# Partial sums of a seven-product pair kept in PSUM banks instead of added one by one

## The chip, the cores and the metric

The kernel runs on one core of a Trainium2 chip. The metric is the device time of one execution in microseconds. Engines are named as in the profile: PE is TensorE (matrix products), PEld its weight loads, DVE VectorE, ACT ScalarE, POOL GpSimd, SP SyncE, which issues most transfers.

## The reference

One layer of a diffusion backbone over 128 context and 1024 latent tokens (T = 1152), width 1024, fp32. Cut to what matters here:

```python
h = rmsnorm(x, g_norm_mix) * (1 + sc1) + sh1
z = h @ w_in                       # latents, gates, q/k/v of the mLSTM, output and branch gates
...                                # latent attention (A) and bidirectional mLSTM (B)
out = (g_a * (att @ w_o_mla) + g_b * (hm @ w_o_mlstm)) @ w_out
x = x + gt1 * out
h = rmsnorm(x, g_norm_ffn) * (1 + sc2) + sh2
a, u = split(h @ w_ffn_in, 2)      # 2 x 2816 features
x = x + gt2 * ((silu(a) * u) @ w_ffn_out)
```

The change concerns `h @ w_in` (all but a few of its columns) and `h @ w_ffn_in`.

## The kernel before

Features lie on the 128 partitions, tokens along the free dimension. Each fp32 operand is split into a high part (`hi`, ACT, line 69) and a low part (`lo`, DVE, line 75), and a product is made of three matmuls, high by high, high by low, low by high (`mm3`, lines 98 to 100).

`pair` (line 1645) computes two tiles of 128 output features for column groups of 576 tokens, as a 2 by 2 block product: the blocks of the weights are two tiles by two halves of K (a11, a12, a21, a22), those of the moving side two halves of K by two halves of 288 tokens (B11 to B22). Seven block products take the place of eight (Winograd's form). The stationary operands, `a` blocks or sums S1 to S4 of them, are formed by `w_ops` (from line 1620): POOL forms the sums (lines 1632, 1633, 1638, 1642, tile `ws`), ACT and DVE split each (tile `wo`, 4 buffers in the first product and 6 in the feed-forward product). The moving operands T1 to T4 and the B blocks are formed once and serve all pairs; for the feed-forward product `h2_ops` does that for one half of the tokens (normalization at line 1572, modulation at 1578, sums on POOL from 1590 on, splits).

The table `ORDER` (line 1616) names what step i of a pair multiplies. In every step, for each column group, twelve matmuls of 128x288 (4 blocks of K, three matmuls each) fill one bank of the pool `mm`, which has six banks in both products. The bank is read by one instruction per sum it enters: the first product is copied by ACT (line 1670, tile `m`), the other six steps add theirs on DVE (helper `add`, line 1658) to what is there, with two additions in step 3, seven in all:

```python
elif i == 1: add(u2[g], m1[g], b)
elif i == 2: add(d[g][1], u2[g], b)
elif i == 3: add(d[g][2], u2[g], b); add(d[g][3], d[g][1], b)
elif i == 4: add(d[g][0], m1[g], b)
elif i == 5: add(d[g][1], d[g][1], b)
else: add(d[g][2], d[g][2], b); done(g)
```

`pair` is called 19 times with two column groups by the first product (`z_lat`, `z_qk`, `z_big`; from 184 to 650 us), and for the 22 pairs of the feed-forward product, each a gate and a value tile: pairs 0 to 5 first for tokens 0 to 575 alone, then for the others alone, while `h2_ops` of the second half of the tokens is still at work, then pairs 6 to 21 with both groups (from 1425 to 1950 us). In `z_big` the outputs are tiles `zo`; `done` takes their sigmoid (line 660) and a DVE multiplication (662). In the feed-forward product they are `sa` and `uu`; `done` takes silu of `sa` (ACT, line 1702), multiplies (POOL, 1703) and stores.

Beside the pairs runs other work, of which `tick` emits a piece per step. In `z_big` it is `background` (line 666), modulation columns: per piece a DVE multiplication with sum (line 700, `mj`), a POOL multiplication (701) and an ACT sum (682, `wm`); at its start and halfway a vector `sr` is loaded and ACT takes its silu (689). The compiler's scheduler then orders the instructions of each engine; each engine works its queue off in order.

## Time and profile before

| what | value |
|---|---|
| median of 3 runs (lowest, highest) | 2245.0 us (2242.07, 2249.43) |
| span of the profiled execution, first to last instruction | 2242.8 us |
| mean granted TensorE clock | 0.966 |
| PE busy | 2083.1 us, 93% |
| DVE busy | 1659.5 us, 74%, 2998 instructions |
| ACT busy | 1068.0 us, 48%, 2225 instructions |
| POOL busy | 1127.2 us, 50% |

The profiled execution lists its span alone; the median of the runs is 2.2 us above it. A busy share is an average over stages in which different engines set the pace; the views by stretch, the waits and the chain tell which one does where.

### The profile page before, as it was taken

Reading aid. Unit: us, or ns where it says so; the run is one execution under the profiler, and the core shown is the slowest. Engines: PE = TensorE matmul, PEld = TensorE weight load, DVE = VectorE, ACT = ScalarE, POOL = GpSimd, SP = SyncE. Lnnn points to the kernel's source line nnn. Section 1 sums busy time; section 2 is a strip of 40 time slices with the busy share of each in tenths; the row PEclk is TensorE's granted clock in tenths of the full one; section 3 lists DMA queues with packets and bytes.
Section 4 is the critical chain, followed back from the end, with each engine's and each line's share of the span. In section 5 each row is a group of like instructions: output and inputs, shape, how many; then the busy total and the mean of one; then the engine's idle time right before and its main releaser. Section 6 shows DMA issues by size and latency. Waiting matters only on the chain.

```text
span 2242.8 us, 40186 instructions
## 1 busy us (share of the span) xinstructions
PE 2083.1 (93%) x14713; PEld 1998.2 (89%) x14713; DVE 1659.5 (74%) x2998; ACT 1068.0 (48%) x2225; POOL 1127.2 (50%) x850
## 2 busy tenths in 40 slices
PE   6799999999989987999999999879999999989898
PEld 2799998999978776998998999879999999989897
DVE  6725745988845879998987666899755565799895
ACT  4322333445445556777776435444322222356464
POOL 3612122667624415877877543677867634431411
PEclk8899999999999998999999999999999999999899
DMA  7121244555479775322224575223555522557664
GB/s 286 63 93 59 90 142 124 164 174 183 152 241 330 238 230 175 90 74 65 84 66 102 170 224 157 86 83 122 186 177 183 175 89 80 161 173 248 206 201 138
DMA packets 234532, 340.97 MB, mean 152 GB/s; under 512 B 18110, under 2 KB 170398, under 8 KB 233310
## 3 DMA queue, kind: packets, MB, share of 16 engines
q1 hardware_dynamic: 225790, 328.73, 46.0%
q0 software_dynamic: 4848, 6.06, 1.1%
q10 hardware_dynamic: 3696, 3.61, 0.5%
q8 instruction: 116, 1.90, 0.4%
q14 instruction: 82, 0.67, 0.1%
HBM read 250.55 MB, written 87.80 MB: 151 GB/s over the span
## 4 chain that ended last, share of the span: by engine, by line
PE 42%; DVE 16%; DMA 7%; POOL 6%; issue 6%; ACT 2%; SPq 1%; DVEq 0%; POOLq 0%; ACTq 0%
PE mm L98 10%; PE mm L100 10%; PE mm L99 10%; DVE wo L75 4%; DMA pr<-w_fo 3%; DVE sm L1374 2%; DVE pl L75 1%; PE st L98 1%; PE pv L1437 1%; PE pv L1438 1%; PE st L100 1%; PE st L99 1%; PE mx L1372 1%; DMA N<-d_nm 1%; PE p L1079 1%
## 5 line engine op out<-in xcount | busy, mean ns | idle before, releaser
L100 PE MATMUL mm<-th,wo 128*128 128x288 f32 x1840 | 546.8, 298 | 14.0 <-DVE wo L75 13.7
L98 PE MATMUL mm<-th,wo 128*128 128x288 f32 x1840 | 547.6, 298 | 2.7 <-DVE zo L1658 1.1
L99 PE MATMUL mm<-tl,wo 128*128 128x288 f32 x1840 | 546.2, 297 | 0.0
L100 PEld LDWEIGHTS mm<-th,wo 128*128 128x128 f32 x1840 | 348.9, 190 | 18.2 <-DVE wo L75 17.6
L75 DVE TENSOR_TENSOR wo<-wr,wo 128x512 fp32r<-128x512 f32 (+1 forms) x317 | 314.6, 1008 | 59.4 <-ACT wo L69 54.4
L98 PEld LDWEIGHTS mm<-th,wo 128*128 128x128 f32 x1840 | 348.2, 189 | 4.5 <-issue 1.6
L99 PEld LDWEIGHTS mm<-tl,wo 128*128 128x128 f32 x1840 | 348.3, 189 | 0.1
L69 ACT ACTIVATE wo<-wr 128x512 fp32r<-128x512 f32 (+1 forms) x317 | 187.5, 607 | 147.9 <-PE mm L100 69.5
L69 ACT ACTIVATE wo<-ws 128x512 fp32r<-128x512 f32 x188 | 116.7, 627 | 271.7 <-PE mm L100 160.5
L75 DVE TENSOR_TENSOR wo<-ws,wo 128x512 fp32r<-128x512 f32 x188 | 186.7, 996 | 62.1 <-ACT wo L69 61.9
L100 PE MATMUL mm<-xh,wo 128*128 128x288 f32 x616 | 184.7, 301 | 10.3 <-DVE wo L75 10.3
L1642 POOL TENSOR_TENSOR ws<-wr,ws 128x512 f32<-128x512 f32 x47 | 62.3, 1326 | 243.5 <-DVE wo L75 238.2
L99 PE MATMUL mm<-xl,wo 128*128 128x288 f32 x616 | 184.7, 300 | 0.0
L98 PE MATMUL mm<-xh,wo 128*128 128x288 f32 x616 | 184.2, 299 | 0.5 <-ACT wo L69 0.5
L1420 POOL TENSOR_TENSOR es<-es,p 128x512 f32<-128x512 f32 (+1 forms) x96 | 129.4, 1348 | 34.8 <-ACT p L1403 19.9
L98 PE MATMUL mm<-B,wo 128*128 128x288 f32 x456 | 134.8, 296 | 2.6 <-DVE zo L1658 1.7
L100 PE MATMUL mm<-B,wo 128*128 128x288 f32 x456 | 134.8, 296 | 0.0
L99 PE MATMUL mm<-B,wo 128*128 128x288 f32 x456 | 134.8, 296 | 0.0
L701 POOL TENSOR_TENSOR wm<-wm,sr 128x512 f32<-128x512 f32 x64 | 100.1, 1567 | 65.2 <-DVE mj L700 49.2
L100 PEld LDWEIGHTS mm<-xh,wo 128*128 128x128 f32 x616 | 118.1, 192 | 12.7 <-DVE wo L75 12.5
L98 PEld LDWEIGHTS mm<-xh,wo 128*128 128x128 f32 x616 | 118.2, 192 | 0.7 <-ACT wo L69 0.7
L99 PEld LDWEIGHTS mm<-xl,wo 128*128 128x128 f32 x616 | 118.4, 192 | 0.0
(443 smaller groups left out, 6076.6 us busy)
## 6 DMA issues: line engine op xcount, KB each, us to landing
wr<-w_ff SPq DMA_DIRECT2D x56, 512.0 KB
wm<-wm SPq DMA_DIRECT2D x32, 512.0 KB
wr<-d_w SPq DMA_DIRECT2D x32, 512.0 KB
d_z<-zo SPq DMA_DIRECT2D x48, 288.0 KB
d_g<-uu SPq DMA_DIRECT2D x44, 288.0 KB
wr<-w_big SPq DMA_DIRECT2D x24, 512.0 KB
wr<-w_fo SPq DMA_DIRECT2D x24, 512.0 KB
pr<-w_fo SPq DMA_DIRECT2D x40, 256.0 KB
```

What stands on the lines that cost most here:

```text
L69: i = self.nc.scalar.activation(out, in_, AF.Copy)
L75: return self.nc.vector.tensor_sub(out, in_, f32v(hi)).ins
L98: mm(out, lhs[0], rhs[0], start=first, stop=False)
L99: mm(out, lhs[0], rhs[1], start=False, stop=False)
L100: self.pe = mm(out, lhs[1], rhs[0], start=False, stop=last).ins
L701: nc.gpsimd.tensor_tensor(w[:, n], w[:, n], sr[:, 1], op=ALU.mult)
L1079: self.pe = mm(p1, A[:, h], V[:, h], start=True, stop=not carried).ins
L1372: nc.tensor.matmul(s[:, :kc], q[0:QK, 0, q0 + t * P:q0 + (t + 1) * P], k[0:QK, 0, k0 + j * kc:k0 + (j + 1) * kc], start=True, stop=True)
L1374: nc.vector.tensor_reduce(sm[:, 3 * t + j:3 * t + j + 1], s[:, :kc], axis=AX.X, op=ALU.max, negate=True)
L1420: G.tensor_tensor(U["sum"][:, :m], U["sum"][:, :m], p[:, :m], op=ALU.add)
L1437: nc.tensor.matmul(pv[:, :n], v[:, i], ph[:, e, :n], start=c + e == 0, stop=False)
L1642: G.tensor_tensor(s4, a12, s2, op=ALU.subtract)
```

## The change

The seven products are computed in another order, and those that are summed anyway accumulate in the same bank. Steps 0, 2, 4 and 6 of a column group share a bank X, steps 1 and 3 a bank Y, step 5 has its own. X and Y are copied out by ACT while they hold a partial sum: X after step 0 (`m`), after step 2 (into output 1) and after step 6 (output 2), Y after step 1 (`y`). DVE adds Y to output 1 after step 3, `y` and X to output 3 after step 4, `m` and step 5's bank to output 0. The matmuls are as many as before.

```diff
-    ORDER = (("A11", "B11"), ("S2", "T2"), ("S1", "T1"), ("S3", "T3"), ("A12", "B21"), ("S4", "B22"), ("A22", "T4"))
+    ORDER = (("A11", "B11"), ("S1", "T1"), ("S2", "T2"), ("S4", "B22"), ("S3", "T3"), ("A12", "B21"), ("A22", "T4"))
...
         yield split(a11)
+        yield split(s1)
         yield split(s2)
-        yield split(s1)
+        s4 = s()
+        G.tensor_tensor(s4, a12, s2, op=ALU.subtract)
+        yield split(s4)
         s3 = s()
         G.tensor_tensor(s3, a11, a21, op=ALU.subtract)
         yield split(s3)
         yield split(a12)
-        s4 = s()
-        G.tensor_tensor(s4, a12, s2, op=ALU.subtract)
-        yield split(s4)
         yield split(a22)
...
+        def keep(to, b, n):
+            to[g] = sp.tile([P, HT], F32, name=self.nm(n), tag="u2", bufs=self.ub)
+            nc.scalar.copy(to[g], b)
...
-                b = self.bank(self.pp, "mm")[:, :HT]
+                if i in (0, 1):
+                    (X, Y)[i][g] = bank()
+                b = bank() if i == 5 else (Y if i in (1, 3) else X)[g]
                 for k in range(4):
-                    self.mm3(b, (w[:, 0, k], w[:, 1, k]), (h[:, k], l[:, k]), k == 0, k == 3)
+                    self.mm3(b, (w[:, 0, k], w[:, 1, k]), (h[:, k], l[:, k]), k == 0 and i in (0, 1, 5), k == 3, skip=True)
                 if i == 0:
-                    m1[g] = sp.tile([P, HT], F32, name=self.nm("m1"), tag="u2", bufs=self.ub)
-                    nc.scalar.copy(m1[g], b)
+                    keep(m1, b, "m1")
                 elif i == 1:
-                    u2[g] = sp.tile([P, HT], F32, name=self.nm("u2"), tag="u2", bufs=self.ub)
-                    add(u2[g], m1[g], b)
+                    keep(y1, b, "y1")
                 elif i == 2:
                     d[g] = dst(g)
-                    add(d[g][1], u2[g], b)
+                    nc.scalar.copy(d[g][1], b)
                 elif i == 3:
-                    add(d[g][2], u2[g], b)
-                    add(d[g][3], d[g][1], b)
+                    add(d[g][1], d[g][1], b)
                 elif i == 4:
+                    add(d[g][3], y1[g], b)
+                elif i == 5:
                     add(d[g][0], m1[g], b)
-                elif i == 5:
-                    add(d[g][1], d[g][1], b)
                 else:
-                    add(d[g][2], d[g][2], b)
+                    nc.scalar.copy(d[g][2], b)
                     done(g)
```

In `h2_ops` the split of B22 moves ahead of that of T3, and the split of B21 ahead of that of T4:

```diff
         split("T2", t1)
+        split("B22", b22)
+        self.free(s22)
         split("T3", b12)
         self.free(s12)
-        split("B22", b22)
-        self.free(s22)
         G.tensor_tensor(t1, b21, t1, op=ALU.subtract)
+        split("B21", b21)
+        self.free(s21)
         split("T4", t1)
         self.free(st1)
-        split("B21", b21)
-        self.free(s21)
```

The second feed-forward product, which has an order of its own, is left alone.

The order of instructions shows the change in three places. First PE, in the feed-forward product's pairs with one column group, late in that part: the first of the twelve matmuls of each step (`mm` with its number is the bank's tile, `th` the moving operand, `wo` the stationary one). Before, one pair:

```order
L98 MATMUL mm_18100<-th_16945,wo_18097 128x288 [waits DVE_49,Activation_49]
...
L98 MATMUL mm_18118<-th_16956,wo_18115 128x288 [waits DVE_49,Activation_49]
...
L98 MATMUL mm_18136<-th_16950,wo_18133 128x288 [waits DVE_49,Activation_49]
...
L98 MATMUL mm_18157<-th_16960,wo_18154 128x288 [waits DVE_49,Activation_49]
...
L98 MATMUL mm_18175<-th_16973,wo_18172 128x288 [waits DVE_49,Activation_49]
...
L98 MATMUL mm_18194<-th_16964,wo_18191 128x288 [waits DVE_49,Activation_49]
...
L98 MATMUL mm_18211<-th_16969,wo_18208 128x288 [waits Activation_49]
```

Now, beginning with step 0 of a pair (tile `mm_17870` is its bank X, `mm_17888` its Y, `mm_17960` its step 5; `mm_17736` is bank X of the pair before, `mm_18004` and `mm_18022` are X and Y of the next):

```order
L98 MATMUL mm_17870<-th_16755,wo_17867 128x288
...
L98 MATMUL mm_17888<-th_16760,wo_17885 128x288 [waits Activation_49]
...
L98 MATMUL mm_17736<-th_16783,wo_17840 128x288 [waits DVE_49]
...
L98 MATMUL mm_17870<-th_16766,wo_17903 128x288 [waits Activation_49]
...
L98 MATMUL mm_17888<-th_16770,wo_17923 128x288 [waits Activation_49]
...
L98 MATMUL mm_17960<-th_16779,wo_17957 128x288
...
L98 MATMUL mm_17870<-th_16774,wo_17941 128x288 [waits Activation_49]
...
L98 MATMUL mm_18004<-th_16755,wo_18001 128x288
...
L98 MATMUL mm_18022<-th_16760,wo_18019 128x288 [waits Activation_49]
...
L98 MATMUL mm_17870<-th_16783,wo_17974 128x288 [waits DVE_49]
```

Before, the steps stand in their own order, each in a new tile. Now step 6 of the pair before comes after step 1, step 5 after step 3, and the next pair's steps 0 and 1 before step 6; between two uses of a bank lie two steps or more. The waits that stand at matmuls of these steps are for ACT and DVE. In the parts with two column groups the steps stay in their own order, each for both groups, with the matmuls of three other group-steps between two uses of a bank.

Second DVE, at the same place. Before, most of one pair (`u` the first sum, `sa` and `uu` the outputs):

```order
L1658 TENSOR_TENSOR u_3451_18131<-m_3448_18113,mm_18118 128x288 [waits PE_49]
L75 TENSOR_TENSOR wo_18236<-wr_18228,wo_18236 128x512 [waits DMAHW4_49,Activation_49]
L1658 TENSOR_TENSOR sa_18149<-u_3451_18131,mm_18136 128x288 [waits DVE_49,PE_49]
L75 TENSOR_TENSOR wo_18254<-ws_18233,wo_18254 128x512 [waits Activation_49]
L1658 TENSOR_TENSOR uu_18150<-u_3451_18131,mm_18157 128x288 [waits DMAHW2_49,PE_49]
L1658 TENSOR_TENSOR uu_18150<-sa_18149,mm_18157 128x288 [waits DVE_49]
L75 TENSOR_TENSOR wo_18272<-ws_18232,wo_18272 128x512 [waits Activation_49]
L1658 TENSOR_TENSOR sa_18149<-m_3448_18113,mm_18175 128x288 [waits PE_49]
L75 TENSOR_TENSOR wo_18293<-ws_18291,wo_18293 128x512 [waits Activation_49]
L1658 TENSOR_TENSOR sa_18149<-sa_18149,mm_18194 128x288 [waits DVE_49,PE_49]
L75 TENSOR_TENSOR wo_18311<-wr_18228,wo_18311 128x512 [waits Activation_49]
L1658 TENSOR_TENSOR uu_18150<-uu_18150,mm_18211 128x288 [waits PE_49]
```

Now:

```order
L1659 TENSOR_TENSOR uu_17785<-y_3247_17767,mm_17736 128x288 [waits DMAHW0_49,PE_49]
L75 TENSOR_TENSOR wo_17941<-ws_17939,wo_17941 128x512 [waits Activation_49]
L75 TENSOR_TENSOR wo_17957<-wr_17859,wo_17957 128x512 [waits DVE_49,PE_49,Activation_49]
L75 TENSOR_TENSOR wo_17974<-wr_17861,wo_17974 128x512 [waits DVE_49,DMAHW2_49,PE_49,Activation_49]
L75 TENSOR_TENSOR wo_18001<-wr_17993,wo_18001 128x512 [waits DMAHW4_49,PE_49,Activation_49]
L75 TENSOR_TENSOR wo_18019<-ws_17997,wo_18019 128x512 [waits PE_49,Activation_49]
L1659 TENSOR_TENSOR sa_17918<-sa_17918,mm_17888 128x288 [waits PE_49]
L75 TENSOR_TENSOR wo_18037<-ws_17998,wo_18037 128x512 [waits Activation_49]
L1659 TENSOR_TENSOR uu_17919<-y_3267_17901,mm_17870 128x288 [waits DMAHW3_49,PE_49]
L1659 TENSOR_TENSOR sa_17918<-m_3264_17883,mm_17960 128x288 [waits PE_49]
L75 TENSOR_TENSOR wo_18057<-ws_18055,wo_18057 128x512 [waits Activation_49]
```

Between the splits of the weights (line 75) seven additions stood per pair; now there are three (line 1659 in the changed kernel), `sa` twice and `uu` once.

Third ACT, in the `z_big` pair in which the second `sr` is loaded. Before (1670 the copy of the first product, one per column group):

```order
L69 ACTIVATE wo_5158<-ws_5156 128x512 [waits PE_49,Activation_49]
L660 ACTIVATE zo_4866<-zo_4866 128x576 [waits DVE_49]
L1670 COPY m_727_5056<-mm_5043 128x288 [waits PE_49]
L1670 COPY m_729_5071<-mm_5058 128x288 [waits PE_49]
L69 ACTIVATE wo_5197<-wr_5032 128x512 [waits Activation_49]
L682 ACTIVATE wm_4945,ms<-wm_4945 128x512 [waits DMAHW4_49,Activation_49,Pool_49]
L682 ACTIVATE wm_4945,ms<-wm_4945 128x512 [waits Pool_49]
L69 ACTIVATE wo_5234<-ws_5232 128x512 [waits PE_49,Activation_49]
L689 ACT_TABLE_LOAD [waits DMAHW2_49]
L689 ACTIVATE sr_5110<-sr_5110 128x1024 [waits DVE_49]
L69 ACTIVATE wo_5271<-wr_5034 128x512 [waits DMAHW1_49,PE_49,Activation_49]
```

Now (1663 copies `m` and `y`, 1682 copies the second partial sum into output 1):

```order
L1663 COPY m_631_4936<-mm_4923 128x288 [waits PE_49]
L682 ACTIVATE wm_4829,ms<-wm_4829 128x512 [waits DMAHW4_49,Pool_49]
L1663 COPY m_633_4951<-mm_4938 128x288 [waits PE_49]
L69 ACTIVATE wo_5073<-ws_5071 128x512
L682 ACTIVATE wm_4829,ms<-wm_4829 128x512 [waits Pool_49]
L1663 COPY y_637_4973<-mm_4960 128x288 [waits PE_49]
L689 ACT_TABLE_LOAD [waits DMAHW2_49]
L689 ACTIVATE sr_4990<-sr_4990 128x1024 [waits DVE_49]
L1663 COPY y_639_4988<-mm_4975 128x288 [waits PE_49]
L69 ACTIVATE wo_5106<-wr_4912 128x512
L1682 COPY zo_5014<-mm_4923 128x288 [waits DMAHW6_49,PE_49]
L1682 COPY zo_5028<-mm_4938 128x288 [waits DMAHW5_49,DMAHW0_49,PE_49]
```

Two copies per pair became eight, of which six stand here; they alternate with instructions that wait for POOL (682), and the silu of `sr` (689), which waits for a load, now stands between the two copies of `y`.

## Rows read from the trace of the kernel before

**Rows 1.** The page's line of busy time by engine (us, share of the span, instructions), and its chain of waits summed by engine.

```profile
PE 2083.1 (93%) x14713; PEld 1998.2 (89%) x14713; DVE 1659.5 (74%) x2998; ACT 1068.0 (48%) x2225; POOL 1127.2 (50%) x850
...
PE 42%; DVE 16%; DMA 7%; POOL 6%; issue 6%; ACT 2%; SPq 1%; DVEq 0%; POOLq 0%; ACTq 0%
```

**Rows 2.** Busy time by stretch: start and end, length, then for PE, PEld, DVE, ACT and POOL the busy us with the instructions in brackets, the granted TensorE clock as a share of full speed, DMA share, GB/s. 440 to 540 is the part of the first product that has background work beside it, 1435 to 1520 the first pairs of the feed-forward product, 1600 to 1920 its later pairs, 1920 to 2000 its end.

```profile
440.00:540.00 100.00, 93.44 (x691) 91.46 (x690) 87.16 (x150) 52.24 (x115) 67.95 (x46) 1.00 0.55 175
490.00:515.00 25.00, 21.73 (x158) 20.86 (x158) 19.14 (x34) 13.70 (x28) 14.96 (x11) 1.00 0.52 163
1435.00:1520.00 85.00, 71.08 (x479) 67.13 (x478) 84.25 (x103) 43.40 (x73) 53.98 (x29) 0.94 0.28 87
1600.00:1920.00 320.00, 318.86 (x2386) 317.95 (x2385) 178.51 (x303) 87.68 (x157) 183.31 (x174) 1.00 0.43 138
1920.00:2000.00 80.00, 70.81 (x504) 68.98 (x503) 69.78 (x66) 38.95 (x64) 41.63 (x16) 0.96 0.60 185
```

**Rows 3.** The same view for the instructions of line 1658 alone, the additions of the partial sums: length, DVE busy us (instructions), clock, DMA share, GB/s.

```profile
440.00:540.00 100.00, 22.77 (x57) 1.00 0.55 175
1435.00:1520.00 85.00, 15.21 (x36) 0.94 0.28 87
1920.00:2000.00 80.00, 7.80 (x18) 0.96 0.60 185
```

**Rows 4.** Instructions of line 1658 (one of its ten groups) and of line 1670, the copy of the first product: count, duration in ns (shortest/median/longest), first and last start.

```profile
L1658 DVE TENSOR_TENSOR u<-m,mm x82: 437/442/456, 188.5 to 1932.2; 128x288 f32<-128x288 f32 x82
...
L1670 ACT COPY m<-mm x82: 375/398/405, 184.7 to 1928.3; 128x288 f32<-128x288 f32 x82
```

**Rows 5.** The chain of waits in 1435 to 1520, its shares by engine and line (the row ends where the view cuts it).

```profile
by line: DVE wo L75 35.0%; issue 19.6%; DVE x L1572 7.4%; DVE tl L75 6.2%; DVE dg L141 5.3%; DVE sa L1658 5.2%; DVE uu L1658 4.7%; PE mm L100 3.7%; PE mm L99 2.7%; PE mm L98 2.7%; DVE u L1658 1.8%; DVE t L122 1.6%; ACT th L69 1.3%; ACT sa L
```

**Rows 6.** What TensorE waited for (us in total, times, longest us), in 440 to 540, in 1435 to 1520 and in 1600 to 1920, in this order, parted by dots.

```profile
PE mm L98 <- DVE zo L1658: 2.8, 3, 1.5
PE mm L100 <- DVE wo L75: 2.8, 4, 1.3
...
PE mm L100 <- DVE wo L75: 10.4, 6, 5.5
...
PE mm L98 <- DVE sa L1658: 0.5, 1, 0.5
```

**Rows 7.** VectorE's instructions with two operands from SBUF in 1435 to 1520, by line and form: count, busy us, mean ns, idle time before them.

```profile
L75 DVE TENSOR_TENSOR wo<-ws,wo 128x512 fp32r<-128x512 f32 x20 | 25.0, 1267 | 0.3 <-ACT wo L69 0.3
L75 DVE TENSOR_TENSOR wo<-wr,wo 128x512 fp32r<-128x512 f32 x15 | 20.6, 1394 | 0.0
L75 DVE TENSOR_TENSOR tl<-x,th 128x1152 fp32r<-128x1152 f32 x4 | 8.5, 2130 | 0.0
L1572 DVE TENSOR_TENSOR x<-x,acc 128x1152 f32<-128x1152 f32 x4 | 6.3, 1623 | 0.0
...
L75 DVE TENSOR_TENSOR tl<-t,th 128x1152 fp32r<-128x1152 f32 x3 | 5.6, 1861 | 0.2 <-ACT th L69 0.2
```

**Rows 8.** The timeline of VectorE and, behind the dots, of GpSimd around 1500: start us, duration us, engine, line, operation (x2: two behind each other).

```profile
1493.89 0.44 DVE L1658 TENSOR_TENSOR u<-m,mm 128x288 f32<-128x288 f32 x1
...
1497.41 3.15 DVE L75 TENSOR_TENSOR wo<-ws,wo 128x512 fp32r<-128x512 f32 x1
...
1504.98 1.34 DVE L75 TENSOR_TENSOR tl<-t,th 128x1152 fp32r<-128x1152 f32 x1
...
1506.62 1.28 DVE L75 TENSOR_TENSOR wo<-ws,wo 128x512 fp32r<-128x512 f32 x2
...
1492.70 2.54 POOL L1703 TENSOR_TENSOR uu<-uu,sa 128x576 f32<-128x576 f32 x1
...
1496.90 3.12 POOL L1600 TENSOR_TENSOR t<-x,t 128x1152 f32<-128x1152 f32 x1
...
1508.04 1.29 POOL L1642 TENSOR_TENSOR ws<-wr,ws 128x512 f32<-128x512 f32 x1 [4.62 <-DVE wo L75]
```

**Rows 9.** What ScalarE waited for (us in total, times, longest us) in 360 to 650 and, behind the dots, in 1420 to 1560.

```profile
ACT wm L682 <- POOL wm L701: 77.5, 48, 3.9
...
ACT L689 <- DMA sr<-cR: 3.6, 1, 3.6
...
ACT sa L1702 <- DVE sa L1658: 26.5, 9, 6.1
ACT wo L69 <- POOL ws L1633: 11.6, 4, 4.2
```

**Rows 10.** The timeline of ScalarE at 498 to 506 and, behind the dots, at 1440 to 1448 (in square brackets the idle time before, and what ended it).

```profile
498.64 1.28 ACT L689 ACT_TABLE_LOAD   x1 [3.58 <-DMA sr<-cR]
499.93 1.06 ACT L689 ACTIVATE sr<-sr 128x1024 f32<-128x1024 f32 x1
500.89 0.61 ACT L69 ACTIVATE wo<-wr 128x512 fp32r<-128x512 f32 x1
503.11 0.63 ACT L682 ACTIVATE wm<-wm 128x512 f32<-128x512 f32 x1 [1.60 <-POOL wm L701]
...
1440.83 0.68 ACT L1702 ACTIVATE sa<-sa 128x576 f32<-128x576 f32 x1 [1.86 <-DVE sa L1658]
...
1445.20 2.19 ACT L1578 ACTIVATE x<-x,mod,A 128x288 f32<-128x288 f32 x4 [2.04 <-DVE x L1572]
...
1447.81 2.17 ACT L1578 ACTIVATE x<-x,mod,A 128x288 f32<-128x288 f32 x4
```

More of the change, by code (lines that the diff above doesn't have):

```diff
@@ L93, in load_w, with mm3 @@
         return (h.rearrange("p (k f) -> p k f", k=kt), l.rearrange("p (k f) -> p k f", k=kt))
-    def mm3(self, out, lhs, rhs, first, last):
+    def mm3(self, out, lhs, rhs, first, last, skip=False):
         mm = self.nc.tensor.matmul
-        mm(out, lhs[0], rhs[0], start=first, stop=False)
-        mm(out, lhs[0], rhs[1], start=False, stop=False)
-        self.pe = mm(out, lhs[1], rhs[0], start=False, stop=last).ins
+        mm(out, lhs[0], rhs[0], start=first, stop=False, skip_group_check=skip)
+        mm(out, lhs[0], rhs[1], start=False, stop=False, skip_group_check=skip)
+        self.pe = mm(out, lhs[1], rhs[0], start=False, stop=last, skip_group_check=skip).ins
     def gemm_tile(self, w, x, evac, pool, tag, chunks=CHUNKS, m=P, f0=0):
@@ L1654, in pair @@
             r.append(t)
-        m1, u2, d = {}, {}, {}
+        m1, y1, d, X, Y = {}, {}, {}, {}, {}
+        bank = lambda: self.bank(self.pp, "mm")[:, :HT]
         def add(*args):
             self.ev = nc.vector.tensor_add(*args).ins
+        def keep(to, b, n):
+            to[g] = sp.tile([P, HT], F32, name=self.nm(n), tag="u2", bufs=self.ub)
+            nc.scalar.copy(to[g], b)
         for i, w in enumerate(self.w_ops(*r)):
```

## The prediction

> **What bounds the kernel now.** I read the page first: TensorE is busy 93% of the span, VectorE 74%, ScalarE 48%, and the chain that ended last lies on TensorE for 42% and on VectorE for 16% of its length [rows 1]. An average like this does not tell what fewer additions are worth, so I read the stretches in which `pair()` runs. They differ. From 1600 to 1920 TensorE is busy 318.9 of 320 us and VectorE only 178.5: there the products set the time, and no VectorE work taken away can show. From 1435 to 1520, the first feed-forward pairs, it is the other way round: VectorE is busy 84.25 of 85 us and TensorE 71.1. From 440 to 540 TensorE is busy 93.4 of 100 us with VectorE at 87; half of the 6.6 us lost lie in 490 to 515, where 21.7 of 25 are busy [rows 2]. From 1920 to 2000 TensorE misses 9.2 us, but only 18 additions still run there, against 36 in 1435 to 1520 and 57 in 440 to 540 [rows 2, 3]. The reader is to see that the change can only pay in the first feed-forward pairs and in the background part of the first product.
>
> What TensorE waits for there agrees: 10.4 us for the low parts of the weights (line 75) in 1435 to 1520; in 440 to 540 2.8 us for those and 2.8 us for additions that had not yet read their bank [rows 6]. In the chain of 1435 to 1520 the additions themselves hold 5.2 + 4.7 + 1.8 = 11.7% [rows 5].
>
> **The change, part by part.** *Removed: four of seven additions per group of columns.* There are 82 such groups [rows 4], so 328 additions. One lasts 0.442 us; where they follow each other the windows book 15.21/36 = 0.42 us for one [rows 3, 4]. In 1435 to 1520 some 36 × 4/7 = 21 go, 21 × 0.42 = **8.7 us** if every one delayed the next weight split. The chain gives the other end: 11.7% of 85 us is 9.9 us, 4/7 of it **5.7 us** [rows 5]. TensorE has room for either: 479 matmuls at the pace of the later pairs (320 us / 2386 = 0.134 us) are 64 us of 85 [rows 2]. I take 7.
>
> In 440 to 540, 57 × 4/7 = 33 additions go, 13 us of VectorE time [rows 3]. The gain is capped by the 6.6 us that TensorE loses, and of the 3.3 us lost in 490 to 515 [rows 2] most belongs to ScalarE, which waits 3.58 us for the load of `sr`, then loads a table for 1.28 us [rows 10]; the change leaves that load where it is. The rest is waits for additions and low parts; both shrink. I take **3 us**, bounds 1 and 6.6. Line 1920 on: VectorE is nearly full only in the part without additions, so 1 us, bounds 0 and 18 × 4/7 × 0.43 = 4.4. Everywhere else nothing: TensorE's own work covers it, and if that cover went it would be VectorE time of 328 × 0.42 = 138 us in all, most of it still beside products.
>
> Where this relief goes is doubtful in one point. Beside GpSimd's 3.12 us subtraction one low part took 3.15 us, while two of them at 1506.62, in the 4.62 us in which GpSimd is idle, took 1.28 together, 0.64 each; an addition (one operand in a bank) took 0.44 us beside GpSimd as well [rows 8]. So what goes is work that GpSimd doesn't slow, and what stays is work that it does. The Trainium skill ("SBUF — State Buffer", section "Who interferes with whom") states it as an exclusive lock: a VectorE instruction with two SBUF inputs and a GpSimd one that reads SBUF block each other, one with at most one SBUF input contends with nobody. The rows agree in direction; by the lock taken strictly the sum would lose the 7 us, which is the first rival below.
>
> *Added: three copies on ScalarE per group*, 246 of 0.40 us [rows 4], 98 us on an engine busy 43 of 85 and 88 of 320 us [rows 2]. Hidden behind products and weight splits in time, but not always in order. *New waits of TensorE:* an accumulating step must not begin before the partial sum is copied out of its bank. In the two-column-group stretches three group-steps of 12 matmuls, 36 × 0.134 = 4.8 us, lie between; in the first feed-forward pairs the order interleaves two pairs, so that at least two, 3.2 us, do. What delays a copy is what stands before it on ScalarE: line 682's wait for GpSimd, 77.5/48 = 1.6 us, longest 3.9 [rows 9], and 0.6 us each of line 682 and a high part [rows 10]; 1.6 + 0.6 + 0.6 + 0.4 = 3.2, inside 4.8, and only the longest waits exceed it, by under 1 us. In one pair the `sr` load sits between the two copies of the second product: 3.58 + 1.28 + 1.06 = 5.9 us [rows 10], up to 1.5 over. In the second feed-forward pair the copy stands behind eight modulations of line 1578, 2.04 + 2.19 + 2.17 us [rows 10], 3 us over, on a stretch where VectorE is late anyway. Behind these copies wait high parts, which VectorE's low parts need. I take **2 us** of new stalls, bounds 0 and 10.
>
> *Moved:* s4 is built and split two steps earlier, B22 and B21 one earlier each: the same GpSimd, ScalarE and VectorE work, no DMA more or less; SP's and GpSimd's queues keep their instructions. Since the whole order shifts, the mLSTM and attention stages between, which the diff does not touch, move by a few places too; I see no reason for a sign and allow 4 us each way, about the 2.9 us between lowest and middle run.
>
> Sum: −7 − 3 − 1 + 2 = **−9 us**. From the profiled span of 2242.8 that is 2233.8; the median of the runs is 2245.0, 2.2 above the span, so **2236**. All of it is to be read against 0.3% (6.7 us), about what a measurement of this kernel can tell from no change.
>
> **The rivals.** *The relief is given back (no change).* In 1435 to 1520 the instructions with two SBUF operands would take, alone, 35 × 0.64 + 7 × 1.34 + 4 × 1.34 = 37 us, the last four being as wide as the seven [rows 7, 8]; with GpSimd's 54 [rows 2] that is 91 us in a stretch of 85. If the two engines exclude each other, these set the stretch, and the additions only filled gaps in which VectorE was held up anyway. Then the 7 us are gone, and −3 − 1 + 2 gives 2243. Against it: GpSimd's rows are themselves lengthened while blocked (so the 91 is too much), and low parts right before additions are on the chain [rows 5]. Chance 0.25.
>
> *Copies late in order (slower).* Silu waits 26.5/9 = 2.9 us, up to 6.1, for its last addition, and high parts wait 11.6/4 = 2.9 us for GpSimd [rows 9]; a copy queued behind one of them comes 2.9 + 0.7 + 0.4 = 4.0 us late, 0.8 beyond the 3.2 us, and after the longest 4. If each of the twelve single-group pairs stalls once for the middle of these, 2.4 us, that is 29 us, in the place of 2; part of it would fall where VectorE is late anyway, so a quarter less, 22: 2245 − 11 + 22 = 2256. It cancels the gain when the new waits reach 11 us. For it: ScalarE's queue is in order, and before the change TensorE's matmuls never depended on it for a bank beyond one copy per group. Against it: from 1600 to 1920 ScalarE is a quarter busy, and where TensorE waited there for an addition it was 0.5 us [rows 2, 6]. Chance of slower by over 0.3%: 0.13.
>
> *More than the additions (faster).* With VectorE out of the way TensorE may recover all its losses in both stretches, 85 − 64 = 21 and 6.6 us: 2217. Needed for that: VectorE must fall by 21 us where 8.7 are taken out, so the low parts must also escape GpSimd. Chance 0.12.
>
> That the change does not do what it says is excluded by the order: three additions and four copies per group, as many matmuls as before.
>
> **How the numbers follow.** The forecast has the remaining 0.50, 2228 to 2243 with the bounds of its terms. Chances: faster by over 0.3% (below 2238.3) 0.12 + 0.40 of the forecast's 0.50 + 0.02 of the first rival = 0.54; slower 0.13 and 0.02 for the unforced shifts of order = 0.15; the rest, 0.31, the same. The range, 2220 to 2251, takes in the forecast, the first rival and the nearer ends of the other two.
>
> **What would show it.** Right: 1435 to 1520 shorter by 5 to 9 us, VectorE still nearly full in it with 15 additions instead of 36; no row of TensorE waiting over 1 us for lines 1663 or 1682; 1600 to 1920 as full as before. The first rival: fewer additions, but low parts with a mean above the present 1.27 and 1.39 us [rows 7] and the stretch as long. The second: TensorE waits for the copies in single-group pairs, 10 us or more in sum. Wrong altogether, if the difference lies in stages that the diff does not touch, or if TensorE is no longer full from 1600 to 1920.

## The result: slower by 0.3% where 0.4% less was forecast

| | before | changed |
|---|---|---|
| median of 15 runs each, taken side by side | 2246.28 us | 2253.78 us |
| ratio, 95% interval | | 1.0029 [1.0015, 1.0042] |
| profiled execution: time, span | span 2242.8 us | 2249.14 us, span 2247.4 us |

One of the 15 runs of the changed kernel is a slow one, of 6950.39 us, and the ratio leaves it out. The forecast was 2236 us, 2220 to 2251. The change does cost time, some 3 to 9 us.

The page of the changed kernel, busy time and chain; they answer to [rows 1].

```profile
PE 2080.7 (93%) x14713; PEld 1999.0 (89%) x14713; DVE 1521.3 (68%) x2670; ACT 1145.9 (51%) x2471; POOL 1132.0 (50%) x850
...
PE 36%; DVE 16%; DMA 9%; POOL 8%; issue 7%; ACT 5%; SPq 1%; DVEq 0%; POOLq 0%; ACTq 0%
```

VectorE lost 138 us of work, as the forecast's 328 × 0.42 said; ScalarE gained 78, where the forecast had 98, in 246 more instructions. The chain moved from TensorE (42 to 36%) to ScalarE (2 to 5%), DMA and GpSimd. The stretches of [rows 2], columns as there:

```profile
440.00:540.00 100.00, 93.43 (x672) 91.99 (x671) 75.71 (x115) 56.51 (x134) 66.73 (x44) 0.97 0.51 164
490.00:515.00 25.00, 22.71 (x161) 22.48 (x159) 18.26 (x27) 15.23 (x35) 15.48 (x12) 0.93 0.55 180
1435.00:1520.00 85.00, 72.73 (x500) 70.60 (x499) 80.27 (x90) 51.24 (x94) 60.21 (x31) 0.93 0.28 88
1600.00:1920.00 320.00, 311.63 (x2313) 309.75 (x2312) 117.46 (x178) 113.47 (x235) 178.94 (x169) 0.99 0.43 137
1920.00:2000.00 80.00, 72.05 (x516) 70.00 (x516) 63.10 (x55) 36.43 (x66) 42.16 (x17) 0.98 0.54 174
```

Read the matmul counts, not the busy time. From 440 to 540 TensorE is as busy as before but did 672 matmuls instead of 691, at a granted clock of 0.97 instead of 1.00. From 1435 to 1520 it did 500 instead of 479, a gain. From 1600 to 1920, where I expected nothing, 2313 instead of 2386.

Since the number of matmuls is the same in all kernels, the n-th matmul of one profile can be set against the n-th of another. The table shows by how many us each profile fell back (+) or drew ahead (−) against the first profile of before, stretch by stretch (times of before; every row is worked out from the starts of the 14713 matmuls in two profiles; the up to 2.5 us by which they differ at 377 are left out).

| profile | first product 377–645 | middle stages 645–1407 | single-group pairs 1407–1612 | two-group pairs 1612–1880 | after 1880 |
|---|---|---|---|---|---|
| before, second profile (e12) | −0.3 | −7.8 | −0.4 | +0.5 | −0.1 |
| changed | +10.9 | −9.3 | −5.0 | +9.8 | −3.9 |
| changed, second profile (e8) | +10.6 | −3.4 | −4.1 | +8.5 | −2.2 |
| e1 first product only | +10.7 | −0.4 | +0.1 | +7.2 | −2.6 |
| e2 feed-forward only | −0.1 | +0.4 | −4.1 | +5.1 | −2.9 |
| e3 sums after copies | +5.2 | +2.3 | −4.2 | +6.6 | −2.6 |
| e4 third sa | +11.1 | +3.5 | −4.5 | +5.6 | −3.8 |
| e5 own tile | +10.8 | +0.9 | −4.9 | +3.7 | −4.3 |
| e6 both moves | +5.0 | −7.1 | −4.4 | +4.0 | −5.2 |
| e7 one vector | +0.2 | −6.4 | −4.3 | +8.3 | −2.7 |
| e9 single-group only | −0.6 | −1.2 | −4.2 | +3.3 | −2.2 |
| e10 all moves | +2.7 | −4.8 | −4.9 | +4.8 | −2.8 |
| e11 before, sr from DRAM | −3.7 | +2.2 | −0.9 | +0.8 | −1.0 |
| e13 one w_fo load | +11.3 | −7.2 | −4.4 | +1.6 | −1.2 |
| e14 single-group, adds put back | +0.2 | +0.8 | +11.9 | −0.5 | −0.6 |
| e15 single-group and sr | −3.7 | −4.1 | −4.3 | +4.3 | −0.7 |

Two losses, 11 us and some 9, stand against a gain of 4 to 5. The middle stages differ by 6 to 8 us between two profiles of the same kernel, so no single profile's total says much. What TensorE waited for in 440 to 540 and, behind the dots, in 1660 to 1850, in the changed kernel (us, times, longest; compare [rows 6]):

```profile
PE mm L98 <- ACT zo L1682: 3.7, 3, 2.0
PE mm L98 <- ACT y L1663: 2.8, 2, 2.3
...
PE mm L98 <- ACT sa L1682: 7.2, 5, 2.0
PE mm L98 <- ACT m L1663: 1.0, 1, 1.0
```

In both places it is a copy on ScalarE that frees a bank. How one of them comes late, on ScalarE's timeline from 423 to 432 and, behind the dots, on GpSimd's and on TensorE's:

```profile
423.84 0.63 ACT L682 ACTIVATE wm<-wm 128x512 f32<-128x512 f32 x1 [1.26 <-POOL wm L701]
...
425.52 0.63 ACT L682 ACTIVATE wm<-wm 128x512 f32<-128x512 f32 x1 [0.67 <-POOL wm L701]
426.05 0.19 ACT L682 ACTIVATION_READ_ACCUMULATOR wm<-wm 128x1 f32 x1
426.15 0.38 ACT L1663 COPY y<-mm 128x288 f32<-128x288 f32 x1
426.43 0.63 ACT L69 ACTIVATE wo<-wr 128x512 fp32r<-128x512 f32 x1
426.96 0.39 ACT L1682 COPY zo<-mm 128x288 f32<-128x288 f32 x1
430.96 0.63 ACT L682 ACTIVATE wm<-wm 128x512 f32<-128x512 f32 x1 [3.62 <-POOL wm L701]
431.50 0.19 ACT L682 ACTIVATION_READ_ACCUMULATOR wm<-wm 128x1 f32 x1
431.59 0.38 ACT L1682 COPY zo<-mm 128x288 f32<-128x288 f32 x1
...
429.22 1.71 POOL L701 TENSOR_TENSOR wm<-wm,sr 128x512 f32<-128x512 f32 x1
...
424.10 0.29 PE L100 MATMUL mm<-th,wo 128*128 128x288 f32 x1
...
432.02 0.40 PE L98 MATMUL mm<-th,wo 128*128 128x288 f32 x1 [2.00 <-ACT zo L1682]
```

The bank of the second column group is full when the matmul of 424.10 is done; its copy, at 431.59, stands behind a sum that waits 3.62 us for GpSimd, whose product ends at 430.93. TensorE starts 0.05 us after that copy ends, having stood for 2.00 us.

Such a wait costs more than its own length. The granted clock behind this one, and behind the two other longest waits for a copy in the first product (2.01 us to 483.45, 2.29 us to 506.61), in the changed kernel; and behind the dots the whole first product from 377 to 645, before and changed:

```profile
433.10:436.40 3.30, 3.30 (x15) 3.30 (x15) 3.30 (x9) 0.06 (x1) 1.66 (x1) 0.50 0.51 159
484.20:487.50 3.30, 3.30 (x16) 3.30 (x15) 3.30 (x9) 0.25 (x1) 1.43 (x1) 0.51 0.47 170
508.20:511.50 3.30, 3.30 (x15) 3.30 (x15) 3.30 (x4) 1.64 (x6) 2.36 (x2) 0.50 0.26 83
...
377.00:645.00 268.00, 261.44 (x1955) 259.14 (x1955) 226.01 (x405) 133.91 (x290) 161.61 (x107) 1.00 0.52 166
...
377.00:645.00 268.00, 256.03 (x1875) 253.00 (x1874) 193.84 (x301) 147.59 (x347) 162.19 (x105) 0.98 0.50 163
```

In each of the three spells TensorE is busy all the time, but at 0.50, the lower of its two levels (1.2 of 2.4 GHz): matmuls start 0.24 us apart instead of 0.13, and some 14 of them lose 1.5 us. So of the 10.9 us lost in the first product some 4.5 are lower clock behind waits, and 5.4 are TensorE standing (12.0 us of 268 not busy, before 6.6). The kernel before had no such spell there. The two-group pairs of the changed kernel have one, at 0.51 from 1740.5 to 1743.8. Its second profile (e8) has two spells in the first product, and none behind the third wait, of 2.32 us.

In 1660 to 1850 ScalarE's two longest waits are these, and behind the dots GpSimd's longest:

```profile
ACT sa L1682 <- POOL uu L1708: 44.4, 13, 6.5
ACT wo L69 <- POOL ws L1641: 25.6, 5, 7.7
...
POOL ps L1733 <- DMA pr<-w_fo: 52.8, 15, 7.2
```

The copy into output 1 (tile `sa`, two buffers) must wait until GpSimd's product of an earlier pair has read that buffer, and GpSimd stands in front of the loads for `prep`, which forms sums of blocks of `w_fo`, the weights of the second feed-forward product. Before, VectorE bore the same wait, at no price, as the kernel before shows in the same stretch:

```profile
DVE sa L1658 <- POOL uu L1703: 24.6, 11, 5.7
```

### The profile page after: what moved, and what is told of

Same layout as the page of the kernel before. It is cut to its first block, busy times and chain, and to the rows that moved or that the text cites. A ratio compares the mean times of both kernels' runs of the same rounds, so it can differ in the third digit from the quotient of the medians.

```text
span 2247.4 us, 39930 instructions
## 1 busy us (share of the span) xinstructions
PE 2080.7 (93%) x14713; PEld 1999.0 (89%) x14713; DVE 1521.3 (68%) x2670; ACT 1145.9 (51%) x2471; POOL 1132.0 (50%) x850
## 4 chain that ended last, share of the span: by engine, by line
PE 36%; DVE 16%; DMA 9%; POOL 8%; issue 7%; ACT 5%; SPq 1%; DVEq 0%; POOLq 0%; ACTq 0%
PE mm L98 9%; PE mm L100 9%; PE mm L99 9%; DVE wo L75 5%; DMA pr<-w_fo 4%; DVE sm L1374 2%; DVE pl L75 2%; PE p L1079 1%; POOL wm L701 1%; PE pv L1438 1%; PE pv L1437 1%; PE p L1084 1%; POOL ps L1737 1%; PE st L98 1%; PE p L1081 1%
## 5 line engine op out<-in xcount | busy, mean ns | idle before, releaser
L75 DVE TENSOR_TENSOR wo<-wr,wo 128x512 fp32r<-128x512 f32 (+1 forms) x317 | 295.8, 953 | 162.5 <-ACT wo L69 154.7
L75 DVE TENSOR_TENSOR wo<-ws,wo 128x512 fp32r<-128x512 f32 x188 | 193.4, 1034 | 151.9 <-ACT wo L69 120.3
L1641 POOL TENSOR_TENSOR ws<-wr,wr 128x512 f32<-128x512 f32 x47 | 67.8, 1442 | 198.3 <-DVE wo L75 198.3
```

The costliest lines, as they stand in the source:

```text
L75: return self.nc.vector.tensor_sub(out, in_, f32v(hi)).ins
L1641: G.tensor_tensor(s3, a11, a21, op=ALU.subtract)
```

## The experiments

Ratios are against runs of the kernel before on the same chip, with 95% intervals.

**e1, e2: one half each.** Edit: `pair`, `w_ops` and `ORDER` in both forms.

```diff
 e1: def ffn_in: ... self.pair_seq([self.a["w_ff"] ...     # the old form, h2_ops as before
 e2: def z_lat, z_qk, z_big: ... self.pair_seq(...          # the old form
```

> Only the pairs of the first product accumulate in banks; the feed-forward pairs stay as before. Theory: TensorE loses 9 to 11 us between 415 and 545 us, because copies wait on ScalarE behind line 682, and the mLSTM and attention stages give most of it back, so the whole is 0 to 6 us slower than before, with TensorE waits for the copies of 8 us or more in 415 to 560. Rival (the loss comes from chance shifts of the order in stages that the diff does not touch): no such waits, and a total within 2 us of before or any other difference that starts after 650 us.

Measured 2262.27 us, 1.0077 [1.0058, 1.0097]. The first product loses 10.7 us, as said, with 9.6 us of waits for copies in 415 to 560, but the middle stages gave nothing back, so the total was worse than I expected. The old two-group pairs lost 7.2 us in this profile as well; its cause stays open.

> Only the feed-forward pairs accumulate in banks; the first product stays as before. Theory: 4 to 5 us gained from 1435 to 1600, 8 to 10 us lost from 1660 to 1850, where the copy into the output tile sa waits on ScalarE for GpSimd to release that tile and holds the bank; the end of the pairs gives back 3 to 4, so the total is 0 to 5 us slower than before. Rival (chance shifts of order): no loss between 1660 and 1850.

Measured 2246.34 us, 1.0003 [0.9991, 1.0014]: −4.1, then +5.1, less than the 8 to 10 that I expected, then −2.9. The feed-forward half of the change is level; the first half is what makes it slower. Chance shifts are out for the first product, which loses 10.6 to 11.3 in each of the six profiles with the changed pairs and no move there, and nothing with the old ones.

**e3: the sums behind the copies.**

```diff
-                with self.tc.issue_after(self.ea):
+                with self.tc.issue_after(self.ec):   # the last copy of a partial sum
                     nc.scalar.activation(t, t, AF.Copy, accum_out=o)
```

> The changed kernel with one thing moved: the background sums of line 682 are ordered behind the last copy of a partial sum, no longer behind the last high part, so that both copies of a step stand ahead of the wait for GpSimd. Theory: TensorE's waits for copies in 415 to 560 fall from 10.0 to under 4 us (the one at the load of sr can stay), the lag that builds up there falls from 11 to under 5 us, and the total falls by 2 to 8 us against the changed kernel. Rival: the lag is the background work's own and stays at 9 us or more, with TensorE waiting for high or low parts in place of the copies.

Measured 2248.26 us, 1.0014 [1.0003, 1.0025]. The loss falls from 10.9 to 5.2 us, just over the 5 named. The order of ScalarE decides half of it. TensorE's waits in 415 to 560 are now:

```profile
PE mm L98 <- ACT y L1663: 4.5, 1, 4.5
PE mm L98 <- DVE zo L1659: 4.0, 2, 2.0
PE mm L100 <- DVE wo L75: 1.0, 2, 0.8
```

**e7: e3 without the second `sr`.**

```diff
-            if i % 16 == 0:
+            if i == 0:
                 sr = self.bp.tile([P, 2, W], F32, name=self.nm("sr"), tag="sr")
```

> The third run's kernel without the second load of the vector sr and its silu: the second half of the modulation columns is computed with the first half of the vector. Theory: of the lag of 5.5 us that is left in 415 to 545, the 4.5 us wait of TensorE for a copy behind that load goes, and the lag at 545 us is 0 to 2 us. Rival: the wait only moves to the next instruction that depends on GpSimd, and 4 us or more stay.

Measured 2245.33 us, 1.0005 [0.999, 1.0021]. The loss of the first product is 0.2 us, 5.0 less than in e3: that much was the one copy of `y` behind the load, table load and silu of `sr`. But the second `sr` costs the kernel before as well: e11 below, which moves it there, draws 3.7 us ahead. Set against e11 the first product of e7 is still 3.9 us behind; TensorE waits 4.0 us for the additions into `zo` that are left. In the changed kernel the piece with `sr` reads (ScalarE, then TensorE):

```profile
503.92 1.28 ACT L689 ACT_TABLE_LOAD   x1 [3.30 <-DMA sr<-cR]
505.21 1.06 ACT L689 ACTIVATE sr<-sr 128x1024 f32<-128x1024 f32 x1
506.18 0.38 ACT L1663 COPY y<-mm 128x288 f32<-128x288 f32 x1
...
506.61 0.40 PE L98 MATMUL mm<-B,wo 128*128 128x288 f32 x1 [2.29 <-ACT y L1663]
```

**e4, e5, e6: the two-group pairs.** e4 gives `sa` (and two tiles elsewhere that share its buffers) three buffers, e5 copies the second partial sum into a tile of its own, e6 is e3 and e5 together.

```diff
 e4: -(("sa", 2), ("uu", 3))   +(("sa", 3), ("uu", 3))
 e5:                elif i == 2:
                    d[g] = dst(g)
-                    nc.scalar.copy(d[g][1], b)
+                    keep(e1, b, "e1")                 # in the feed-forward pairs
                elif i == 3:
-                    add(d[g][1], d[g][1], b)
+                    add(d[g][1], e1[g], b)
```

> The changed kernel with three buffers of the output tile sa instead of two, so that the copy into it need not wait for GpSimd's multiplication of the pair before. Theory: TensorE's 7.2 us of waits for the copy into sa in 1660 to 1850 fall under 1 us, the 10 us lost there go, and the total falls by 4 to 9 us against the changed kernel. Rival: GpSimd itself is late there (its sums for the next weights), so that TensorE then waits for low parts instead and the total stays within 2 us.

Measured 2257.37 us, 1.005 [1.0033, 1.0067]; 5.6 us lost in the two-group pairs. That is within what the other profiles without this edit show (5.1 to 9.8), and the copies into `sa` still waited 36.9 us for GpSimd, against 44.4; TensorE's waits for them fell to 3.0 us, not under 1. A third buffer is no cure.

> The changed kernel, but in the feed-forward pairs the second partial sum is copied by ScalarE into a tile of its own (two more buffers of the tile that holds the first and second copies), and the addition after step 3 writes the output tile sa. No copy then waits for GpSimd to release sa; VectorE does, one step later. Theory (a held copy holds bank X and with it TensorE): TensorE's waits for that copy in 1660 to 1850 are gone, the loss of 6 to 10 us there shrinks to 0 to 4, the total falls by 4 to 8 us against the changed kernel. Rival (GpSimd is late with the next weights, held up by the loads of w_fo, whichever engine adds the sums; the first-product-only kernel lost 7 us there with the old pairs): the loss stays at 5 us or more, TensorE waiting for other copies or weights instead.

Measured 2252.54 us, 1.0044 [1.0028, 1.0061]. The loss is 3.7 us, where the changed kernel lost 9.8 and 8.5, and the waits for the copy into `sa` are gone; in 1660 to 1850 TensorE waits for

```profile
PE mm L98 <- ACT m L1663: 3.0, 2, 1.5
PE mm L98 <- DVE uu L1659: 1.6, 1, 1.6
```

The total does not fall by the 4 to 8 us named; in the profiled run the middle stages lost 0.9 us, where they drew ahead by 9.3 and 3.4 in the changed kernel's.

> The changed kernel with both moves: the background sums behind the copies (as in the third run) and the own tile of the fifth. If both waits are the cause of the loss, it is 4 to 10 us faster than the changed kernel and level with the kernel before or up to 4 us faster; if only the first counts, 3 to 4 us faster than the changed kernel; with neither, as the changed kernel.

Measured 2249.49 us, 1.0025 [1.0009, 1.004]: both stretches improve (5.0 and 4.0 us lost), the total, by the ratios, by 1 us where I said 4 to 10.

**e13: the loads of `w_fo` behind the two-group pairs.** The changed kernel issues 48 of them, as the one before (the 44 below is a miscount), two for each of 24 blocks; the edit leaves one block.

```diff
 def prep:
+                if p == 0 and c0 == 0:               # load r once
                     r = sp.tile([P, 2, 2, 256], F32, name=self.nm("pr"), tag="pr")
```

> The changed kernel with one load of w_fo where there are 44: all sums that GpSimd forms for the second product's weights are made from that one block. Theory (GpSimd stands waiting for these loads, with its multiplications uu and weight sums queued behind, and so ScalarE's copies): TensorE loses under 2 us in 1660 to 1850 instead of 8 to 10, and its waits for the copy into sa go. Rival (the copies are late whatever GpSimd waits for): 5 us or more are lost.

One run, 2246.16 us. The loss is 1.6 us, inside the 2 named. TensorE and, behind the dots, ScalarE in 1660 to 1850:

```profile
PE mm L98 <- ACT sa L1682: 2.7, 4, 1.2
...
ACT sa L1682 <- POOL uu L1708: 33.8, 12, 6.2
```

The copies still wait for GpSimd, 33.8 us in sum, but not so long that the bank is missed. That the waits would go was wrong. That the late loads make them too long is what this one run points to: 1.6 us stands outside the 5.1 to 9.8 of the others without a move there, but inside the −0.5 to 7.2 of the old pairs, and the edit also lightens the DMA engines' work (busy share 0.33 in 1612 to 1880, in the changed kernel 0.46).

**e8, e12: second profiles** of the changed kernel and of before, one run each.

> The changed kernel once more, for a second profile. In the first one the granted clock stayed at full speed in 1150 to 1230 us, where the kernel before and three of the runs above show it at 0.91 to 0.94. If that is chance of one execution, this profile shows the lower clock there and a time of 2253 to 2261 us with the lag of the first product kept to 1400 us; if the changed order itself keeps the clock up, it shows full speed and some 2249 us again.

> The kernel before once more, for a second profile. Two stretches are to be compared: 1660 to 1850 us, where every variant lost 4 to 9 us against the first profile of before, the one with the old pairs too; and 1140 to 1230 us, where the granted clock differed between profiles. If the first profile was typical, TensorE is again busy 188 us or more in 1660 to 1850.

2254.0 and 2239.05 us. The two losses came again in e8 (+10.6, +8.5); before again lost nothing in 1660 to 1850. The granted clock in 1150 to 1235 was (before, before again, changed, changed again):

```profile
1150.00:1235.00 85.00, 78.88 (x496) 73.35 (x495) 64.87 (x136) 55.09 (x126) 60.50 (x56) 0.90 0.34 86
...
1150.00:1235.00 85.00, 79.89 (x544) 74.71 (x542) 68.60 (x144) 61.05 (x140) 65.53 (x60) 0.96 0.35 90
...
1150.00:1235.00 85.00, 79.72 (x559) 74.79 (x558) 72.07 (x156) 59.64 (x141) 70.33 (x60) 1.00 0.37 96
...
1150.00:1235.00 85.00, 79.94 (x539) 75.15 (x538) 70.07 (x156) 58.67 (x137) 67.63 (x56) 0.96 0.38 97
```

So a difference of this size in the middle stages comes from one execution to the next, and one profile of each kernel cannot put it down to the change.

**e9, e14: is the gain of the single-group pairs VectorE time?** e9 keeps the change there alone; e14 puts four additions back.

```diff
 e9:        (self.pair if len(groups) == 1 else self.pair_seq)([self.a["w_ff"] ...
 e14: +        def extra(t, b):                         # after each copy, single-group pairs
      +            z = sp.tile([P, HT], F32, name=self.nm("ex"), tag="ex")
      +            nc.vector.tensor_add(z, t, b)
```

> Only the twelve feed-forward pairs with one column group accumulate in banks; the first product and the feed-forward pairs with two groups stay as before. Theory (the two-group pairs lose because a bank is tied to a copy, the single-group pairs gain from fewer additions): 4 to 5 us gained from 1435 to 1600 as in the second run, 0 to 2 us lost from 1660 to 1850, total 3 to 6 us faster than before. Rival (the two-group loss is chance of the order and of the loads of w_fo): 5 us or more are lost from 1660 to 1850 here too, and the total is level with before.

Measured 2241.65 us, 0.9993 [0.9979, 1.0006]: −4.2 us in these pairs, +3.3 in the two-group ones, old form. Between theory and rival; the total cannot be told from before.

> The ninth run's kernel (bank accumulation in single-group pairs alone) with four additions put back per such pair, of a bank and its copy into a scratch tile that nobody reads: VectorE's load is that of before. Theory (the gain there is VectorE time): the 4 to 5 us gained from 1435 to 1600 go to 0 or turn into a loss. Rival (it comes from the interleaved order of the pairs): 3 us or more of the gain stay.

One run, 2258.6 us: 11.9 us lost in these pairs, 16 more than e9. This run does not part the theory from its rival, the interleaved order: VectorE is busy only 70.45 us in 1435 to 1520, so what was lost is not its time. The additions put back also hold the banks that TensorE wants, and its granted clock is 0.85 there; in 1420 to 1525 it waits for

```profile
PE mm L100 <- DVE wo L75: 6.9, 6, 2.5
PE mm L98 <- DVE uu L1660: 5.9, 2, 3.7
...
PE mm L98 <- DVE ex L1668: 3.4, 3, 2.2
```

**e10, e11, e15: what can be kept.** The second `sr` is made at the start, stored, and only loaded halfway; e10 with all moves, e11 in the kernel before, e15 with e9.

```diff
+            if i == 0: (for f in (1, 0): load, silu; for f = 1 also) nc.sync.dma_start(d, sr)
+            elif i == 16: nc.sync.dma_start(sr, d)
```

> The changed kernel with the sums behind the copies, the own tile, and the second sr made at the start, kept in DRAM and only loaded halfway, so that no silu and no table load stand among the copies. Theory: the lag at 545 us is 0 to 2 us (as in the run with one vector), the two-group pairs lose 4 us, the single-group pairs gain 4 to 5: 0 to 5 us faster than before. Rival: the load halfway now holds VectorE and GpSimd, and 3 us or more of the lag stay.

Measured 2241.33 us, 0.9999 [0.9982, 1.0016]: with these moves the change is level with before. It is not level with before plus the same move of `sr` (e11, next): against that its first product is 6.4 us behind, though no copy holds TensorE there any more. From 377 to 645 it waits 5.3 us for additions into `zo` and 2.1 for low parts, against 0.9 and 2.7 in e11.

> The kernel before with the second sr from DRAM alone, as control of the tenth run. Of the 3.3 us that TensorE lost in 490 to 515 most should go: 1 to 3 us faster than before. If the load itself (not the silu and its table loads behind it) is what holds, nothing changes.

Measured 2240.53 us, 0.9986 [0.9972, 1.0001], 3.7 us less in 377 to 645.

> Bank accumulation in single-group pairs alone, and the second sr from DRAM: the two parts that gained without loss in the runs before. If they add up, 3 to 7 us faster than before (ratio 0.997 to 0.9985); if the middle stages level them, no difference.

Measured **2237.74 us, 0.9965 [0.9948, 0.9983]**: faster than the kernel before. It uses the change in 12 of the 82 groups of columns, and the move of `sr`; neither alone could be told from before (e9, e11).

## Why the prediction was wrong

*The additions.* Their number and price were right (VectorE 138 us less). Wrong in size: the 7 us in the single-group pairs measured 4.1 to 5.0, below my lower bound of 5.7. VectorE is no longer full there, 80.27 of 85 us; it now waits for high parts, and ScalarE, which makes them, waits for TensorE to release weight tiles (1435 to 1520, VectorE's waits, then ScalarE's):

```profile
DVE wo L75 <- ACT wo L69: 4.2, 5, 1.5
...
ACT wo L69 <- PE mm L100: 12.1, 6, 4.6
```

The additions of 1435 to 1520 and the low parts there, in the changed kernel:

```profile
1435.00:1520.00 85.00, 7.82 (x18) 0.93 0.28 88
...
L75 DVE TENSOR_TENSOR wo<-ws,wo 128x512 fp32r<-128x512 f32 x24 | 28.5, 1204 | 3.5 <-ACT wo L69 3.5
L75 DVE TENSOR_TENSOR wo<-wr,wo 128x512 fp32r<-128x512 f32 x15 | 21.4, 1449 | 0.7 <-ACT wo L69 0.6
L75 DVE TENSOR_TENSOR tl<-x,th 128x1152 fp32r<-128x1152 f32 x4 | 8.6, 2142 | 0.0
...
L75 DVE TENSOR_TENSOR tl<-t,th 128x1152 fp32r<-128x1152 f32 x3 | 6.2, 2076 | 0.0
```

They are 7.4 us less than the 15.2 of before [rows 3], and 4.2 us of VectorE's time went idle in their place. GpSimd took nothing back: 46 low parts in 64.7 us are 1.41 us each, as the 42 of before in 59.7 us, 1.42 [rows 7]; in e2, e9 and e10 they are 1.40 to 1.45. That settles the first rival: the additions had not only filled gaps. The rival went with the Trainium skill's lock rule ("SBUF — State Buffer", section "Who interferes with whom"), by which a VectorE instruction with two SBUF inputs and a GpSimd one that reads SBUF exclude each other; the 4 to 5 us gained speak against the reading that such exclusion set this stretch, not against the rule. That the gain is VectorE time rather than the interleaved order of the pairs agrees with these rows, but no run parts the two.

*The step that failed* is the one on the added copies: "I take 2 us of new stalls, bounds 0 and 10". In the first product the change cost 11 us. Where the text had "everywhere else nothing: TensorE's own work covers it", the two-group feed-forward pairs lost 5.1 to 9.8 us in the five profiles without a move there (changed twice, e2, e3, e7; mean 7.7), and −0.5 to 7.2 in the seven with the old pairs (mean 2.2): 5.5 us more, with ranges that overlap. Together that is 16 us, against at most 10 allowed. 11 + 5.5 less 4.5 in the single-group pairs, and less some 2 that come back after 1880, is 10 us; the medians differ by 7.5.

Three errors made it. I counted one wait of line 682 (the mean, 1.6 us), one sum and one high part before a copy, "3.2, inside 4.8", and let only the longest waits exceed it, "by under 1 us". Between the filling of the bank after 424.10 and its copy at 431.59 there stood two sums, with waits of 0.67 and 3.62 us, a high part and three other copies: 7 us, and TensorE stood 2.00. The waits do not simply add; the last one ended when GpSimd had done, so what counts is when the latest of the things ahead of the copy can run. That the order behind the sums is the cause is shown by e3, for 5.7 of the 10.9 us. Second, I looked at what stands ahead of a copy, not at what the copy itself needs: its output tile. The wait for `sa` was visible before the change as VectorE's (24.6 us) and cost nothing; I put that down to the bank, which was one of six, so that the next step took another. With a tile of its own for the copy (e5) 3.7 us were lost there. Third, the sum had no term for the clock, which came to 4.5 us in the first product and 1.5 in the two-group pairs of the profiled run.

*The 3 us gain in 440 to 540* did not come in any variant with the changed pairs (best: +0.2 in e7, which is 3.9 behind e11). The waits for additions that I counted there were replaced by waits for copies and for the additions that are left (4.0 us in e3). That most of the 3.3 us in 490 to 515 belongs to the load of `sr` was right: moving it gave the kernel before 3.7 us.

*The rivals.* The second named the mechanism, copies late in ScalarE's order, but put it in the single-group pairs, where TensorE waited 0.2 us for a copy (1435 to 1520),

```profile
PE mm L98 <- ACT y L1663: 0.2, 1, 0.2
```

and gave it 0.13. The third, more than the additions, did not show anywhere.

*The middle stages.* I allowed 4 us each way for shifted order; two profiles of one kernel already differ by 6 to 8 us there. That hid part of the loss in the profiled run, and may be what spreads the runs.

What stays open: why the old two-group pairs lost 3 to 7 us in e1, e9 and e15 and under 1 us in both profiles of before, e11 and e14; how much of the single-group gain is VectorE time; and why the profiles whose two-group pairs ran late gain 2 to 5 us after 1880 (all but e13 and e15, with 1.2 and 0.7), so that the forecast's 1 us there can be neither confirmed nor denied.

## What to carry to other kernels

Accumulating over steps in one bank makes the copy of a partial sum a deadline: before moving such a copy to an engine with time to spare, read what stands ahead of it in that engine's queue and when the latest of it can run, and see whether the tile it writes is free. An engine's idle share (ScalarE's was 52%) says nothing on that. Where a variant takes away a cost that the old kernel also pays (here the second `sr`), its control is the old kernel with the same edit. A change that pays only where one engine is full can be confined to that stretch: 12 of the 82 groups gave all the 4 to 5 us that it gained, though in the total this showed only together with the move of `sr`.

## What the runs showed of the hardware that I had not expected

In the changed kernel's first product three waits of TensorE, of 2.00 to 2.29 us, were each followed by 3.3 us at half the clock (0.50, 0.51 and 0.50), which cost some 1.5 us each and in which TensorE reads as fully busy. Waits as long were not always followed by one: behind 1.99 us in e3 and 2.32 us in e8 the clock stayed at 1.00.

The granted clock in one stretch of the same program differs between executions: 0.90 and 0.96 for before, 1.00 and 0.96 for the changed kernel in 1150 to 1235 us, with 496, 544, 559 and 539 matmuls done there. A busy share hides this, 78.88 to 79.94 of 85 us in all four; the matmul count does not.
